# Casting the x windows on GpSimd's DMA queue and cutting the last loads and stores of a windowed matmul

**Chip and metric.** One core of a Trainium2 chip. Time is device microseconds of one execution, median of several; all runs quoted here are of the fast state (none is over 1.5% above the fastest of its kernel). The profile's span is about 1.7 us shorter than the time.

## The reference

```python
B, S, D, W = 4, 4096, 4096, 64
x: (4, 4096, 4096) fp32    w: (4096, 4096) fp32    offsets: (4,) int64, drawn at random
for b in range(B):
    o = int(offsets[b])
    results.append(x[b, o:o+W] @ w)        # 64 x 4096 by 4096 x 4096
return np.stack(results).astype(np.float32)
```

All of w (67 MB) has to be read once, and 1 MB of x per batch.

## The kernel before

The rows of two batches share the 128 partitions: `xpair[g]` holds batch 2g in partitions 0 to 63 and batch 2g+1 in 64 to 127. TensorE transposes them into fp16 `xT`. w comes as 64 tiles of 128 rows by 2048 columns, cast to fp16 by the DMA, on GpSimd's queue (67.1 MB of w read, 33.6 MB written by that queue on the page). Half of the columns is finished at a time, in eight PSUM tiles of 128x512. At most eight of GpSimd's loads are in flight, since each waits for the one eight places before (in the trace eight are issued by 6.0 us, the ninth at 6.99, when a w tile has landed).

```python
for b in range(B):                                   # x: fp32, 64 partitions each, two queues
    g, m = divmod(b, 2)
    eng = nc.sync if (b % 2 == 0) else nc.scalar
    eng.dma_start(out=xpair[g][m * WIN : (m + 1) * WIN, :],
                  in_=x[b][bass.ds(off_vals[b], WIN), :])
# ... transposes in fp32, copies PSUM -> xT (fp16) on VectorE ...
for c in range(2):
    for ki in range(n_k):                            # 32 tiles of w
        wh = wh_pool.tile([P, NH], fp16, name="wh", tag="wh")
        nc.gpsimd.dma_start(out=wh[:], in_=w[ki*KT:(ki+1)*KT, c*NH:(c+1)*NH])
        # ... 8 matmuls of 128x512 ...
    for g in range(G):
        # ... 4 copies PSUM -> stage, then two stores of 64 partitions each:
        for m in range(2):
            st_eng = nc.sync if (m == 0) else nc.scalar
            st_eng.dma_start(out=out[2*g+m][:, c*NH:(c+1)*NH],
                             in_=stage[m * WIN : (m + 1) * WIN, :])
```

Of the kernel before, what the change touches and what calls it, by code (L numbers as in the profile page):

```python
# [1 line left out]

# [5 lines left out]


@with_exitstack  # L10
def kernel(
    ctx: ExitStack,
    tc: tile.TileContext,
    x: bass.AP,
    w: bass.AP,
    offsets: bass.AP,
    out: bass.AP,
):
    nc = tc.nc
    fp32 = mybir.dt.float32  # L20
    fp16 = mybir.dt.float16

    B, S, D = x.shape
    _, N = w.shape
    WIN = out.shape[1]
    P = 128
    KT = 128
    NT = 512
    NH = N // 2
    n_k = D // KT  # L30
    n_half_sub = NH // NT
    G = B // 2

    SP = mybir.EngineType.SP
    ACT = mybir.EngineType.Activation

    const_pool = ctx.enter_context(tc.tile_pool(name="const", bufs=1))
    x_pool = ctx.enter_context(tc.tile_pool(name="xp", bufs=1))
    wh_pool = ctx.enter_context(tc.tile_pool(name="wh", bufs=18))
    st_pool = ctx.enter_context(tc.tile_pool(name="st", bufs=2))  # L40
    psum_pool = ctx.enter_context(tc.tile_pool(name="ps", bufs=1, space=bass.MemoryType.PSUM))

    identity = const_pool.tile([P, P], fp32, name="identity")
    off_t = const_pool.tile([1, B], mybir.dt.int64, name="off_t")

    xpair = [x_pool.tile([P, D], fp32, name=f"xpair{g}") for g in range(G)]
    xT = [x_pool.tile([P, D], fp16, name=f"xT{g}") for g in range(G)]

    acc = [psum_pool.tile([P, NT], fp32, name=f"acc{a}") for a in range(2 * n_half_sub)]

    nc.sync.dma_start(out=off_t[:], in_=offsets[None, :])
    make_identity(nc, identity[:])

    off_i32 = off_t.bitcast(mybir.dt.int32)
    off_vals = [
        nc.values_load(
            off_i32[0:1, 2 * b : 2 * b + 1],
            engines=[SP, ACT],
            min_val=0,
            max_val=S - WIN,  # L60
        )
        for b in range(B)
    ]

    for b in range(B):
        g, m = divmod(b, 2)
        eng = nc.sync if (b % 2 == 0) else nc.scalar
        eng.dma_start(
            out=xpair[g][m * WIN : (m + 1) * WIN, :],
            in_=x[b][bass.ds(off_vals[b], WIN), :],  # L70
        )

    for g in range(G):
        for j in range(2 * n_half_sub):
            for q in range(4):
                k = 4 * j + q
                nc.tensor.transpose(  # L77
                    out=acc[j][:, q * KT : (q + 1) * KT],
                    in_=xpair[g][:, k * KT : (k + 1) * KT],
                    identity=identity[:],  # L80
                )
            nc.vector.tensor_copy(  # L82
                out=xT[g][:, j * NT : (j + 1) * NT], in_=acc[j][:]
            )

    for c in range(2):
        for ki in range(n_k):
            wh = wh_pool.tile([P, NH], fp16, name="wh", tag="wh")
            nc.gpsimd.dma_start(  # L89
                out=wh[:],  # L90
                in_=w[ki * KT : (ki + 1) * KT, c * NH : (c + 1) * NH],
            )
            for g in range(G):
                for j in range(n_half_sub):
                    a = g * n_half_sub + j
                    nc.tensor.matmul(  # L96
                        out=acc[a][:],
                        lhsT=xT[g][:, ki * KT : (ki + 1) * KT],
                        rhs=wh[:, j * NT : (j + 1) * NT],
                        start=(ki == 0),  # L100
                        stop=(ki == n_k - 1),
                    )
        for g in range(G):
            stage = st_pool.tile([P, NH], fp32, name="stage", tag="stage")
            for j in range(n_half_sub):
                a = g * n_half_sub + j
                if c == 1 and g == 1:
                    nc.vector.tensor_copy(  # L108
                        out=stage[:, j * NT : (j + 1) * NT], in_=acc[a][:]
                    )  # L110
                else:
                    nc.scalar.copy(  # L112
                        out=stage[:, j * NT : (j + 1) * NT], in_=acc[a][:]
                    )
            for m in range(2):
                b = 2 * g + m
                st_eng = nc.sync if (m == 0) else nc.scalar
                st_eng.dma_start(
                    out=out[b][:, c * NH : (c + 1) * NH],
                    in_=stage[m * WIN : (m + 1) * WIN, :],  # L120
                )


# [1 line left out]
_INS = ['x', 'w', 'offsets']  # L125
_OUTS = [((4, 64, 4096), 'float32')]


# [23 lines left out]
```

## Time and profile before

| | before |
|---|---|
| time | 200.42 us (200.12 to 201.49) |
| first DMA traffic | 2.5 us |
| w tile 4 landed | 34.1 us |
| last w tile landed | 184.4 us |
| end of the span | 198.1 us |

"Tile 4 landed" is read from GpSimd: its load of tile 12 was held by the landing of tile 4. I use it as the mark at which x is through and w is alone. The rest of the reading stands in the prediction. One more view is wanted for later: the DMA in one-microsecond windows of the end. The columns are the stretch, its length, busy time of PE, PEld, DVE, ACT and POOL, granted clock, DMA share and GB/s.

```profile
190.00:191.00 1.00, 0.00 (x0) 0.00 (x0) 0.00 (x0) 0.00 (x0) 0.00 (x0) 0.50 0.95 229
192.00:193.00 1.00, 0.00 (x0) 0.00 (x0) 0.00 (x0) 0.00 (x0) 0.00 (x0) 0.50 0.87 246
```

Only stores move here, and the engines read nearly full (0.95 and 0.87) at 229 and 246 GB/s, little more than half of the 426 at which w is read.

### The profile page before, as it was taken

The page shows a single profiled execution, that of the slowest core. Times are in us where ns is not written, and L with a number is a line of the kernel's source. Part 1 is how long each engine was busy: PE and PEld are TensorE (multiplying, and loading weights), DVE is VectorE, ACT ScalarE, POOL GpSimd, SP SyncE. Part 2 cuts the span into 40 slices and gives each one's busy share as a digit, 9 for nine tenths or more (in the row PEclk, how much of TensorE's full clock was granted, in tenths as well). Part 3 has the DMA queues.
Part 4 walks back from the last instruction along what each step waited for, and adds up shares of the span by engine and source line. Part 5 has one row for each costly group of instructions (what it writes and reads, how often), then busy time and mean ns, then how long its engine had stood idle before and what let it go on. Part 6 is the DMA issues. An engine that isn't in the chain of part 4 may idle for free.

```text
span 198.1 us, 1402 instructions
## 1 busy us (share of the span) xinstructions
PE 131.4 (66%) x576; PEld 60.9 (31%) x576; DVE 12.9 (7%) x20; ACT 7.4 (4%) x13; POOL 34.6 (17%) x70
## 2 busy tenths in 40 slices
PE   0000949999987777777770859977777687777500
PEld 0000939444433333333320324433333233333100
DVE  0000648100000000000000000000000000000400
ACT  1100000000000000000052000000000000000400
POOL 8301002211222222221221111222222131000000
PEclk9999987999999999999998599999999999999955
DMA  4999999999999999999999999999999999999194
GB/s 69 247 257 218 239 210 213 213 214 213 213 213 215 213 213 213 214 213 213 213 215 268 352 228 214 213 214 213 213 212 214 213 214 213 214 214 203 22 235 174
DMA packets 10183, 42.02 MB, mean 212 GB/s; under 512 B 1218, under 2 KB 1218, under 8 KB 9410
## 3 DMA queue, kind: packets, MB, share of 16 engines
q0 software_dynamic: 9216, 33.56, 84.7%
q1 hardware_dynamic: 482, 4.19, 8.0%
q10 hardware_dynamic: 480, 4.19, 7.3%
q8 instruction: 4, 0.07, 0.1%
q14 instruction: 1, 0.01, 0.0%
HBM read 71.30 MB, written 4.19 MB: 381 GB/s over the span
## 4 chain that ended last, share of the span: by engine, by line
DMA 89%; POOL 2%; issue 2%; DVE 1%; PE 1%; DVEq 0%; POOLq 0%
DMA wh<-in_w_dram 89%; POOL wh L89 2%; DVE stage L108 1%; PE acc L96 1%; DVEq L147 0%; POOL identity masks.py:199 0%; POOL identity masks.py:197 0%; POOLq masks.py:199 0%; POOLq L89 0%; DVEq L108 0%; POOLq L147 0%; POOLq L136 0%
## 5 line engine op out<-in xcount | busy, mean ns | idle before, releaser
L96 PE MATMUL acc<-wh,xT 128*128 128x512 f16 x512 | 120.3, 383 | 32.0 <-DMA wh<-in_w_dram 32.0
L96 PEld LDWEIGHTS <-xT 128*128 128x128 f16 x512 | 50.2, 98 | 101.8 <-issue 47.3
L89 POOL DMA_DIRECT2D wh<-in_w_dram x64 | 34.0, 534 | 130.5 <-DMA wh<-in_w_dram 122.2
L77 PE MATMUL acc<-identity,xpair 128*128 128x128 f32 x64 | 11.2, 358 | 22.9 <-DMA xpair<-in_x_dram 22.9
L77 PEld LDWEIGHTS acc<-identity,xpair 128*128 128x128 f32 x64 | 10.8, 194 | 23.1 <-issue 23.1
L112 ACT COPY stage<-acc 128x512 f32<-128x512 f32 x12 | 6.2, 600 | 175.1 <-PE acc L96 175.0
L108 DVE COPY stage<-acc 128x512 f32<-128x512 f32 x4 | 2.5, 683 | 150.2 <-PE acc L96 150.2
L82 DVE CAST xT<-acc 128x512 f16<-128x512 f32 x16 | 10.4, 686 | 25.2 <-PE acc L77 25.1
L112 ACT ACT_TABLE_LOAD x1 | 1.3, 1283 | 4.4 <-issue 4.4
masks.py:199 POOL TENSOR_SCALAR_AFFINE_SELECT identity<-identity 128x128 f32<-128x128 f32 x1 | 0.3, 305 | 0.1
masks.py:197 POOL MEMSET identity<- 128x128 f32 x1 | 0.2, 206 | 0.3 <-POOLq L136 0.3
L136 POOL MEMSET const-float32-0.0<- 128x1 f32 x1 | 0.1, 98 | 0.3 <-issue 0.3
L136 POOL MEMSET const-bfloat16-1.0<- 128x1 bf16 x1 | 0.1, 102 | 0.0
L136 POOL MEMSET const-uint8-127<- 128x1 uint8 x1 | 0.1, 102 | 0.0
L136 POOL MEMSET const-float32-1.0<- 128x1 f32 x1 | 0.1, 98 | 0.0
## 6 DMA issues: line engine op xcount, KB each, us to landing
wh<-in_w_dram POOLq DMA_DIRECT2D x64, 512.0 KB, 19.2
xpair<-in_x_dram ACTq DMA_DIRECT2D x2, 1024.0 KB, 20.1
xpair<-in_x_dram SPq DMA_DIRECT2D x2, 1024.0 KB, 19.4
out_dram<-stage SPq DMA_DIRECT2D x4, 512.0 KB, 7.2
out_dram<-stage ACTq DMA_DIRECT2D x4, 512.0 KB, 8.6
off_t<-in_offsets_dram SPq DMA_DIRECT2D x1, 0.0 KB
```

What stands on the lines that cost most here:

```text
L77: nc.tensor.transpose(out=acc[j][:, q * KT : (q + 1) * KT], in_=xpair[g][:, k * KT : (k + 1) * KT], identity=identity[:],)
L82: nc.vector.tensor_copy(out=xT[g][:, j * NT : (j + 1) * NT], in_=acc[j][:])
L89: nc.gpsimd.dma_start(out=wh[:], in_=w[ki * KT : (ki + 1) * KT, c * NH : (c + 1) * NH],)
L96: nc.tensor.matmul(out=acc[a][:], lhsT=xT[g][:, ki * KT : (ki + 1) * KT], rhs=wh[:, j * NT : (j + 1) * NT], start=(ki == 0), stop=(ki == n ...
L108: nc.vector.tensor_copy(out=stage[:, j * NT : (j + 1) * NT], in_=acc[a][:])
L112: nc.scalar.copy(out=stage[:, j * NT : (j + 1) * NT], in_=acc[a][:])
L136: nc = _bacc.Bacc("TRN2", target_bir_lowering=False, num_devices=1)
```

## The change

It intends to shorten the two ends. At the start: two w tiles are issued first, x is cast to fp16 on its way in (it moves to GpSimd's queue, which w's casting loads use, and GpSimd then has to read the offsets, 2.8 to 5.4 us in its trace), and the transposes become fp16 matmuls against an identity. At the end: the last four row blocks of w come as 1024-column halves, so that half of the remaining columns is stored while the other half still loads. All stores become one 128-partition DMA for each pair of batches.

```diff
+    for ki in range(2):
+        pre[(0, ki)] = wh_pool.tile([P, NH], fp16, name="w2048", tag="w2048")
+        nc.gpsimd.dma_start(out=pre[(0, ki)][:], in_=w[ki*KT:(ki+1)*KT, 0:NH])
     make_identity(nc, identity[:])              # now fp16
-            engines=[SP, ACT],
+            engines=[mybir.EngineType.Pool],    # who reads the offsets
...
-        eng.dma_start(                          # x, into fp32 xpair
+        nc.gpsimd.dma_start(                    # x, into fp16 xpair
...
-                nc.tensor.transpose(out=..., in_=xpair..., identity=identity[:])
+                nc.tensor.matmul(out=..., lhsT=xpair..., rhs=identity[:], start=True, stop=True)
...
+    def store(g, c0, cw, stage):
+        eng = nc.sync if g == 0 else nc.scalar
+        eng.dma_start(out=out[2*g:2*g+2].rearrange("b r c -> (b r) c")[:, c0:c0+cw], in_=stage[:])
+    NQ = 1024
+    LAST = 4
     for c in range(2):
+        n_full = n_k if c == 0 else n_k - LAST
...
+        for h in range(NH // NQ):               # second half of the columns only
+            for ki in range(n_full, n_k):
+                wq = load(ki, NH + h * NQ, NQ)
+                # 4 matmuls
+            for g in range(G):                  # g = 0 copied by ScalarE, g = 1 by VectorE
+                # 2 copies, then store(g, NH + h * NQ, NQ, stage)
```

More of the change, by code (lines that the diff above doesn't have):

```diff
@@ L41 @@
     psum_pool = ctx.enter_context(tc.tile_pool(name="ps", bufs=1, space=bass.MemoryType.PSUM))
-    identity = const_pool.tile([P, P], fp32, name="identity")
+    identity = const_pool.tile([P, P], fp16, name="identity")
     off_t = const_pool.tile([1, B], mybir.dt.int64, name="off_t")
-    xpair = [x_pool.tile([P, D], fp32, name=f"xpair{g}") for g in range(G)]
+    xpair = [x_pool.tile([P, D], fp16, name=f"xpair{g}") for g in range(G)]
     xT = [x_pool.tile([P, D], fp16, name=f"xT{g}") for g in range(G)]
@@ L51 @@
     nc.sync.dma_start(out=off_t[:], in_=offsets[None, :])
+    pre = {}
+    for ki in range(2):
+        pre[(0, ki)] = wh_pool.tile([P, NH], fp16, name="w2048", tag="w2048")
+        nc.gpsimd.dma_start(
+            out=pre[(0, ki)][:], in_=w[ki * KT : (ki + 1) * KT, 0:NH]
+        )
     make_identity(nc, identity[:])
@@ L66 @@
         g, m = divmod(b, 2)
-        eng = nc.sync if (b % 2 == 0) else nc.scalar
-        eng.dma_start(
+        nc.gpsimd.dma_start(
             out=xpair[g][m * WIN : (m + 1) * WIN, :],
@@ L76 @@
                 k = 4 * j + q
-                nc.tensor.transpose(
+                nc.tensor.matmul(
                     out=acc[j][:, q * KT : (q + 1) * KT],
-                    in_=xpair[g][:, k * KT : (k + 1) * KT],
-                    identity=identity[:],
+                    lhsT=xpair[g][:, k * KT : (k + 1) * KT],
+                    rhs=identity[:],
+                    start=True,
+                    stop=True,
                 )
@@ L84, with load, mm @@
             )
-    for c in range(2):
-        for ki in range(n_k):
-            wh = wh_pool.tile([P, NH], fp16, name="wh", tag="wh")
-            nc.gpsimd.dma_start(
-                out=wh[:],
-                in_=w[ki * KT : (ki + 1) * KT, c * NH : (c + 1) * NH],
-            )
+    def load(ki, c0, cw):
+        t = wh_pool.tile([P, cw], fp16, name=f"w{cw}", tag=f"w{cw}")
+        nc.gpsimd.dma_start(out=t[:], in_=w[ki * KT : (ki + 1) * KT, c0 : c0 + cw])
+        return t
+    def mm(a, ki, rhs):
+        nc.tensor.matmul(
+            out=acc[a][:],
+            lhsT=xT[a // n_half_sub][:, ki * KT : (ki + 1) * KT],
+            rhs=rhs,
+            start=(ki == 0),
+            stop=(ki == n_k - 1),
+        )
@@ new lines, in store @@
+    def store(g, c0, cw, stage):
+        eng = nc.sync if g == 0 else nc.scalar
+        eng.dma_start(
+            out=out[2 * g : 2 * g + 2].rearrange("b r c -> (b r) c")[:, c0 : c0 + cw],
+            in_=stage[:],
+        )
+    NQ = 1024
+    LAST = 4
+    for c in range(2):
+        n_full = n_k if c == 0 else n_k - LAST
+        for ki in range(n_full):
+            wh = pre[(c, ki)] if (c, ki) in pre else load(ki, c * NH, NH)
+            for a in range(2 * n_half_sub):
+                j = a % n_half_sub
+                mm(a, ki, wh[:, j * NT : (j + 1) * NT])
+        if c == 0:
@@ L93 @@
             for g in range(G):
+                stage = st_pool.tile([P, NH], fp32, name="stage", tag="stage")
                 for j in range(n_half_sub):
-                    a = g * n_half_sub + j
-                    nc.tensor.matmul(
-                        out=acc[a][:],
-                        lhsT=xT[g][:, ki * KT : (ki + 1) * KT],
-                        rhs=wh[:, j * NT : (j + 1) * NT],
-                        start=(ki == 0),
-                        stop=(ki == n_k - 1),
-                    )
@@ L103 @@
-        for g in range(G):
-            stage = st_pool.tile([P, NH], fp32, name="stage", tag="stage")
-            for j in range(n_half_sub):
-                a = g * n_half_sub + j
-                if c == 1 and g == 1:
-                    nc.vector.tensor_copy(
-                        out=stage[:, j * NT : (j + 1) * NT], in_=acc[a][:]
-                    )
-                else:
-                    nc.scalar.copy(
-                        out=stage[:, j * NT : (j + 1) * NT], in_=acc[a][:]
-                    )
-            for m in range(2):
-                b = 2 * g + m
-                st_eng = nc.sync if (m == 0) else nc.scalar
-                st_eng.dma_start(
-                    out=out[b][:, c * NH : (c + 1) * NH],
-                    in_=stage[m * WIN : (m + 1) * WIN, :],
-                )
+                    nc.scalar.copy(
+                        out=stage[:, j * NT : (j + 1) * NT],
+                        in_=acc[g * n_half_sub + j][:],
+                    )
@@ new lines @@
+                store(g, 0, NH, stage)
+            continue
+        for h in range(NH // NQ):
+            js = range(h * NQ // NT, (h + 1) * NQ // NT)
+            for ki in range(n_full, n_k):
+                wq = load(ki, NH + h * NQ, NQ)
+                for g in range(G):
+                    for j in js:
+                        r = j * NT - h * NQ
+                        mm(g * n_half_sub + j, ki, wq[:, r : r + NT])
+            for g in range(G):
+                stage = st_pool.tile([P, NQ], fp32, name="stq", tag="stq", bufs=4)
+                copy = nc.scalar.copy if g == 0 else nc.vector.tensor_copy
+                for j in js:
+                    r = j * NT - h * NQ
+                    copy(out=stage[:, r : r + NT], in_=acc[g * n_half_sub + j][:])
+                store(g, NH + h * NQ, NQ, stage)
```

## The prediction

> **What bounds the kernel now.** I read the page first: engines, slices, queues, chain.
>
> ```profile
> span 198.1 us, 1402 instructions
> PE 131.4 (66%) x576; PEld 60.9 (31%) x576; DVE 12.9 (7%) x20; ACT 7.4 (4%) x13; POOL 34.6 (17%) x70
> DMA  4999999999999999999999999999999999999194
> GB/s 69 247 257 218 239 210 213 213 214 213 213 213 215 213 213 213 214 213 213 213 215 268 352 228 214 213 214 213 213 212 214 213 214 213 214 214 203 22 235 174
> DMA 89%; POOL 2%; issue 2%; DVE 1%; PE 1%; DVEq 0%; POOLq 0%
> ```
>
> The DMA row is full from the second slice to the 37th, then empty for one slice, then partly busy. The chain is 89% DMA. TensorE is busy two thirds of the time and waits for w. So the time is: start of the DMA, plus all the work queued on it until the last w tile lands, plus a tail. I priced these three.
>
> The steady price of a w tile comes from the chain in order of time. Every hop is a load issued when the load eight places earlier landed.
>
> ```profile
> 61.94 19.14 DMA wh<-in_w_dram
> 81.61 19.13 DMA wh<-in_w_dram
> 101.27 24.11 DMA wh<-in_w_dram
> 125.91 19.13 DMA wh<-in_w_dram
> ```
>
> From 61.94 to 81.61 is 19.67 us for eight tiles, 2.46 us each. A tile is 128x2048 values, 1.05 MB read as fp32 (0.52 MB written as fp16), so w is read at 426 GB/s. The hop at 101.27 holds the stores of the first half of the columns: 24.11 - 19.13 = 5.0 us for 2.1 MB, 420 GB/s. Stores that interleave with w cost about their bytes.
>
> Now the start. GpSimd's timeline: from the ninth load on, each issue marks the landing of tile 0, 1, 2 and so on.
>
> ```profile
> 1.27 0.66 POOL L89 DMA_DIRECT2D wh<-in_w_dram  x1 [0.32 <-issue]
> 6.99 0.53 POOL L89 DMA_DIRECT2D wh<-in_w_dram  x1 [0.99 <-DMA wh<-in_w_dram]
> 18.77 0.53 POOL L89 DMA_DIRECT2D wh<-in_w_dram  x1 [11.24 <-DMA wh<-in_w_dram]
> 29.45 0.53 POOL L89 DMA_DIRECT2D wh<-in_w_dram  x1 [10.15 <-DMA wh<-in_w_dram]
> 31.64 0.53 POOL L89 DMA_DIRECT2D wh<-in_w_dram  x1 [1.67 <-DMA wh<-in_w_dram]
> 34.08 0.53 POOL L89 DMA_DIRECT2D wh<-in_w_dram  x1 [1.91 <-DMA wh<-in_w_dram]
> ```
>
> Tiles 1 to 4 land between 7.0 and 34.1: 27.1 us for four tiles that should take 9.8. The other 17.3 us went to x, which shares the DMA engines. In half-microsecond windows the DMA becomes active at 2.5 us; from there to 7.0 is 4.5 us with one tile in it, so 2.0 us more (slow first moments included). The four x loads, 4.19 MB, cost 19.3 us: 217 GB/s, half the rate of w. The DMA row reads full all the while. A busy share does not show that a transfer is slow.
>
> The tail, from the timeline of the end:
>
> ```profile
> 184.45 1.89 PE L96 MATMUL acc<-wh,xT 128*128 128x512 f16 x8 [0.55 <-DMA wh<-in_w_dram]
> 184.86 2.05 ACT L112 COPY stage<-acc 128x512 f32<-128x512 f32 x4 [79.43 <-PE acc L96]
> 185.78 2.48 DVE L108 COPY stage<-acc 128x512 f32<-128x512 f32 x4 [150.18 <-PE acc L96]
> 186.94 1.82 SPq L118 DMA_DIRECT2D out_dram<-stage  x2
> 186.95 1.86 ACTq L118 DMA_DIRECT2D out_dram<-stage  x2
> ```
>
> The last tile lands at 184.4. Eight matmuls and four DVE copies reach 188.3, then 2.1 MB of stores go out alone, about 280 GB/s from 188.0 to 195.6, and the end is 198.1: 13.7 us after the last tile.
>
> [...] Each x load fills 64 partitions. [...] The trace cannot confirm a gain: interleaved half stores already cost 420 GB/s, alone 280.
> [...] Here 2.5 us lie between the last visible traffic (195.6) and the end, so I keep 2.5.
>
> **The change, part by part.**
>
> *x becomes a casting load on GpSimd's queue.* The bytes read stay 4.19 MB; those written into SBUF halve. Read side: four loads of 1.05 MB at the w price of 2.46 us are 9.8 us. [...] I take 10.7 us (estimate) against 19.3: **-8.6 us**, all of it on the path, as the DMA never idles before the last tile.
>
> *Two w tiles go first, and the offsets are read by GpSimd.* The first load is issued before the identity memset, at about 0.8 instead of 1.27: **-0.4 us**. GpSimd must then build the identity and read four offsets before it can issue x. Beside it lies the price of that on SyncE: first read at 1.9, first x issue at 4.64, so 2.7 us for four reads with checks.
>
> ```profile
> L56 SPq TENSOR_LOAD <-off_t x4: 268/272/463, 1.9 to 3.9; - x4
> ```
>
> If GpSimd reads as fast: two w issues to about 2.1, identity to about 3, reads to 5.8, first x issue there, its data 1.2 us later (as the first w: 1.27 to 2.5), at 7.0. The two w tiles, from 2.1 on with a slow first half microsecond, last 4.9 us and end at about 7.5. The hole is covered, barely. I allow **+0.8 us** for the slow start and a small hole.
>
> *fp16 transposes as plain matmuls.* TensorE's 11.2 us of them fall by several us and the first real matmul moves from 34 to about 23 us. Worth **0**: w paces the rest. TensorE needs 8 x 0.236 = 1.9 us per tile against 2.46, so it catches up in either kernel, and with 18 buffers no load waits on it in the built order before the buffers come round.
>
> *The last four rows of tiles come as half-width tiles, first half of the columns complete before the second.* Eight DMAs of half the bytes, as many descriptors each: I take **+0.2 us**. The stores of the first half, 1.05 MB, now fall largely into the last w loads and push them back by their bytes at 420 GB/s: **+2.5 us** before the last tile. After it: the third of four matmuls ends at about +0.9, two DVE copies of 0.65 reach +2.2, the store is issued there and its data flow 1.1 us later (186.94 to 188.0 before), at +3.3, ACT's own half from +2.6. 1.05 MB in all at 350 GB/s (between 280 and 420) is 3.0 us, to about +5.6, then 2.5 to the end: **+8.1**. Tail: 0.2 + 2.5 + 8.1 = 10.8 against 13.7, **-2.9 us**.
>
> *Merged stores in mid-kernel:* same bytes among w traffic already at 420 GB/s, **0**.
>
> Sum: -8.6 - 0.4 + 0.8 - 2.9 = -11.1 us. The change is thus mostly the x loads, although the diff spends most of its lines on the tail. 200.42 - 11.1 = 189.3; I say 189.2.
>
> **The rivals.**
> 1. *x stays slow.* If the 217 GB/s came [...] from how x lies in HBM, or from three queues alternating in large packets, the cast may not cure it. For it: both halves were in flight at once[...]. Against it: w is read with strides at full rate in the same stretch[...]. Cost: 19.3 again, time about 197.8, within 2%. If x shows 3.4 us a load, halfway: 192.
> 2. *A hole after the two early tiles.* GpSimd may be slower at reading offsets than SyncE, and the x issues sit behind it in one order with everything else; each us more than planned is a us lost, at most some 3: 192. For it: my plan has half a microsecond to spare.
> 3. *The tail gives nothing.* If the first half's stores just delay w and the last stores run at 280 [...], the tail is 12 to 13: 191. Conversely, if they mostly flow after the last tile while TensorE and the copies run, the 2.5 shrinks to 1: 187.5.
> 4. *TensorE becomes the bound* because PE starts with a backlog: 1.9 against 2.46 us a tile, so no.
>
> **Range and chances.** The x term carries the spread: 9.8 to about 14 us, -1 to +3. The tail adds -1.5 to +1.5, the start -0.5 to +1.5. They are independent enough that not all go one way: 186.3 to 193.3. Faster by over 2% means under 196.4, which needs rival 1 in full or several together: 0.95 for faster, 0.04 for within 2%, 0.01 for slower.
>
> **What would show each step.** In the changed profile: x landing near 10, 12, 15 and 17 us, and the first w load that waits for an x load issued soon after each (right if x takes 2.5 to 2.8 us a load, wrong at 4 or more); the DMA busy near 7 us without a gap; tile 4 landed near 26 instead of 34; w still at 2.46 us a tile; the mid hop still about 24 us; the last w tile near 179 and the end about 8 us after. The prediction is wrong if x keeps about 217 GB/s on its read side, or if a gap opens ahead of x.

## The result and the profile after

| | before | after |
|---|---|---|
| time, median | 200.32 us (15 runs) | 186.48 us (8 runs, 185.79 to 187.08) |
| ratio, 95% interval | 1 | 0.9309 (0.9287 to 0.9330) |
| tile 4 landed | 34.1 | 28.2 |
| last w tile landed | 184.4 | 178.8 |
| from there to the end | 13.7 | 6.4 |

Ratios are formed from the fast runs of the same rounds, so they are not quite the ratio of the medians. The kernel gained 13.8 us where 11.1 had been worked out: inside the range, close to its lower end. The ends gained in other shares than predicted.

The page of the changed kernel:

```profile
span 185.2 us, 1385 instructions
DMA  3999999999999999999999999999999999999975
GB/s 55 211 189 210 208 212 216 213 213 214 214 212 214 214 214 212 212 212 213 214 216 246 358 257 215 213 214 212 213 213 214 213 215 212 212 211 208 208 268 228
```

The empty slice near the end is gone. At the start, GB/s is the flat 210 of a casting load instead of 218 to 257. That is not slower: with the cast, the bytes written are counted, half of those read (33.6 MB on the page before for the 67.1 MB of w). GpSimd's timeline, where each x load's landing now releases a w load:

```profile
1.37 1.19 POOL L55 DMA_DIRECT2D w<-in_w_dram  x2 [0.80 <-POOLq L162]
13.52 0.53 POOL L96 DMA_DIRECT2D w<-in_w_dram  x1 [2.75 <-DMA xpair<-in_x_dram]
15.98 0.53 POOL L96 DMA_DIRECT2D w<-in_w_dram  x1 [1.94 <-DMA xpair<-in_x_dram]
18.41 0.53 POOL L96 DMA_DIRECT2D w<-in_w_dram  x1 [1.90 <-DMA xpair<-in_x_dram]
21.53 0.53 POOL L96 DMA_DIRECT2D w<-in_w_dram  x1 [2.60 <-DMA xpair<-in_x_dram]
28.24 0.53 POOL L96 DMA_DIRECT2D w<-in_w_dram  x1 [1.93 <-DMA w<-in_w_dram]
```

The x loads land 2.4 to 3.1 us apart, close to a w tile's 2.46. But the first lands at 13.5, not near 10, and the first w load was issued no earlier than before (1.37 against 1.27). The timeline of the end:

```profile
175.37 5.35 SPq L110 DMA_DIRECT2D out_dram<-stq  x2
...
178.88 1.02 PE L100 MATMUL acc<-w,xT 128*128 128x512 f16 x4 [0.24 <-DMA w<-in_w_dram]
...
179.72 1.29 DVE L146 COPY stq<-acc 128x512 f32<-128x512 f32 x2 [3.73 <-PE acc L100]
181.04 0.34 ACTq L110 DMA_DIRECT2D out_dram<-stq  x1
```

and the same end in windows:

```profile
176.50:177.00 0.50, 0.50 (x3) 0.19 (x2) 0.00 (x0) 0.00 (x0) 0.00 (x0) 1.00 1.06 311
177.50:178.00 0.50, 0.38 (x2) 0.19 (x2) 0.00 (x0) 0.00 (x0) 0.00 (x0) 1.00 1.00 373
180.00:180.50 0.50, 0.00 (x0) 0.00 (x0) 0.50 (x2) 0.36 (x1) 0.00 (x0) 1.00 0.14 57
182.00:183.00 1.00, 0.00 (x0) 0.00 (x0) 0.00 (x0) 0.00 (x0) 0.00 (x0) 0.99 1.01 410
```

The first half's stores are issued at 175.4 and 176.0, flow from 176.3 on (GB/s climbs over w's 210) and are nearly through by 180. The final stores move at 410 GB/s, where the kernel before had 229 and 246 in the windows shown above, 361 at most. Two things thus happened in the tail, an overlap and a faster store, and the trace alone does not share the gain out between them. Nor does it say whether x got cheaper by the cast, the queue or the order.

### The profile page after: what moved, and what is told of

It reads as the page before. It is cut to its first block, busy times and chain, and to the rows that moved or that the text cites. A ratio compares the mean times of both kernels' runs of the same rounds, so it can differ in the third digit from the quotient of the medians.

```text
span 185.2 us, 1385 instructions
## 1 busy us (share of the span) xinstructions
PE 128.4 (69%) x576; PEld 56.1 (30%) x576; DVE 12.3 (7%) x20; ACT 7.4 (4%) x13; POOL 38.8 (21%) x78
## 3 DMA queue, kind: packets, MB, share of 16 engines
HBM read 71.30 MB, written 4.19 MB: 408 GB/s over the span
## 4 chain that ended last, share of the span: by engine, by line
DMA 89%; issue 5%; POOL 1%; POOLq 1%; PE 0%; DVE 0%; DVEq 0%
DMA w<-in_w_dram 89%; POOLq L63 1%; POOL w L55 1%; PE acc L100 0%; DVE stq L146 0%; POOL xpair L74 0%; DVEq L173 0%; POOL w L96 0%; POOLq L74 0%; POOL identity masks.py:197 0%; POOLq L96 0%; POOLq masks.py:199 0%; POOLq L173 0%; POOLq L162 0%
## 5 line engine op out<-in xcount | busy, mean ns | idle before, releaser
L100 PE MATMUL acc<-w,xT 128*128 128x512 f16 x512 | 122.6, 386 | 33.6 <-DMA w<-in_w_dram 33.4
L96 POOL DMA_DIRECT2D w<-in_w_dram x66 | 34.8, 528 | 126.5 <-DMA w<-in_w_dram 113.5
L83 PE MATMUL acc<-identity,xpair 128*128 128x128 f16 x64 | 6.0, 280 | 17.9 <-DMA xpair<-in_x_dram 15.8
L146 DVE COPY stq<-acc 128x512 f32<-128x512 f32 x4 | 2.6, 686 | 151.8 <-PE acc L100 151.8
L83 PEld LDWEIGHTS <-xpair 128*128 128x128 f16 x64 | 5.6, 129 | 18.0 <-issue 18.0
L90 DVE CAST xT<-acc 128x512 f16<-128x512 f32 x16 | 9.7, 680 | 16.9 <-PE acc L83 16.9
L127 ACT COPY stage<-acc 128x512 f32<-128x512 f32 x8 | 4.0, 626 | 92.8 <-PE acc L100 92.8
L146 ACT COPY stq<-acc 128x512 f32<-128x512 f32 x4 | 2.1, 588 | 79.3 <-PE acc L100 79.3
L74 POOL DMA_DIRECT2D xpair<-in_x_dram x4 | 2.1, 518 | 3.1 <-issue 2.9
L55 POOL DMA_DIRECT2D w<-in_w_dram x2 | 1.2, 598 | 0.8 <-POOLq L162 0.8
## 6 DMA issues: line engine op xcount, KB each, us to landing
w<-in_w_dram POOLq DMA_DIRECT2D x60, 512.0 KB, 19.3
out_dram<-stage SPq DMA_DIRECT2D x1, 1024.0 KB, 11.1
```

Of the source, the lines that this page charges most:

```text
L55: nc.gpsimd.dma_start(out=pre[(0, ki)][:], in_=w[ki * KT : (ki + 1) * KT, 0:NH])
L74: nc.gpsimd.dma_start(out=xpair[g][m * WIN : (m + 1) * WIN, :], in_=x[b][bass.ds(off_vals[b], WIN), :],)
L83: nc.tensor.matmul(out=acc[j][:, q * KT : (q + 1) * KT], lhsT=xpair[g][:, k * KT : (k + 1) * KT], rhs=identity[:], start=True, stop=True,)
L90: nc.vector.tensor_copy(out=xT[g][:, j * NT : (j + 1) * NT], in_=acc[j][:])
L96: nc.gpsimd.dma_start(out=t[:], in_=w[ki * KT : (ki + 1) * KT, c0 : c0 + cw])
L100: nc.tensor.matmul(out=acc[a][:], lhsT=xT[a // n_half_sub][:, ki * KT : (ki + 1) * KT], rhs=rhs, start=(ki == 0), stop=(ki == n_k - 1),)
```

## The experiments

Eleven kernels ran, in three groups, each group on one chip with its own runs of the kernel before. All results were correct. Differences in us below are the ratio applied to the 200.3 us of before.

**1. The start alone.** The kernel before with the first three hunks of the diff; its w loop, copies and stores are as before.

```diff
-            wh = wh_pool.tile(...); nc.gpsimd.dma_start(out=wh[:], ...)
+            wh = pre[(c, ki)] if (c, ki) in pre else <the same tile and load>
```

> The start of the change (two early w tiles, x cast to fp16 on GpSimd's queue, fp16 transposes) with the tail and stores of before. My reading of the two traces: the start is worth what tile 4 gained, 34.1 to 28.2, so -5.9 us: 194.5 us, with the last 13.7 us unchanged. The recorded prediction's share for the start was -8.2 us: 192.1. Rival: the gain of the start is taken back later and only the tail counts: 199 or more.

193.14 us, ratio 0.9646 (0.9614 to 0.9678): -7.1 us. Tile 4 landed at 27.7, the last tile at 177.7 (184.4 before), and the end came 13.4 us later. So the start keeps all its gain to the end. It is worth somewhat more than I had read from one trace: there the fourth x load took 3.1 us, here all four landed 2.4 to 2.5 us apart (12.96, 15.40, 17.89, 20.32). Tile 4 shows only 6.4 of the 7.1 us, as the landings are not even. Tile 7 shows them all; its landing in the kernel before, here, and in run 4 below:

```profile
42.12 0.53 POOL L89 DMA_DIRECT2D wh<-in_w_dram  x1 [2.62 <-DMA wh<-in_w_dram]
35.04 0.53 POOL L100 DMA_DIRECT2D w<-in_w_dram  x1 [1.93 <-DMA w<-in_w_dram]
34.96 0.53 POOL L94 DMA_DIRECT2D wh<-in_w_dram  x1 [2.78 <-DMA wh<-in_w_dram]
```

**2. The end alone.** The start of before, the w loop and stores of the change.

```diff
-        wh = pre[(c, ki)] if (c, ki) in pre else load(ki, c * NH, NH)   # of the changed kernel
+        wh = load(ki, c * NH, NH)                                       # x, offsets, transposes as before
```

> The start of before, with the half-width last tiles and merged stores of the change. My reading: from the last w tile to the end 6.4 us instead of 13.7, and the last tile only 0.3 us later: -7.0 us, 193.3 us. The recorded prediction's share for the tail was -2.9: 197.4. Rival, that the two parts need each other (a smaller gain apart than together): e1 and e2 would sum to clearly less than 13.8 us.

193.28 us, ratio 0.9650 (0.9619 to 0.9681): -7.0 us. The two parts sum to -14.1, against -13.8 for the whole change: within the intervals they are independent. This run also prices the tail cleanly, as its tile 4 landed at 34.1, exactly where it did before. From its chain of waits in order of time (start, duration, what):

```profile
175.00 9.74 DMA w<-in_w_dram
184.78 0.82 PE acc L92 x3
```

The last tile landed at 184.7, 0.3 us later than in the kernel before (184.4), although 1.05 MB of stores had been issued ahead of it. From there to the end of its span, 191.5, are 6.8 us.

**3. Merged stores alone.**

```diff
-            for m in range(2):
-                st_eng.dma_start(out=out[2*g+m][:, cols], in_=stage[m*WIN:(m+1)*WIN, :])
+            st_eng = nc.sync if (g == 0) else nc.scalar
+            st_eng.dma_start(out=out[2*g:2*g+2].rearrange("b r c -> (b r) c")[:, cols], in_=stage[:])
```

> Only the stores change against before: one 128-partition store for each pair of batches in place of two 64-partition stores on two queues. Theory, that half-partition stores are slow: the final 2.1 MB go at about 400 GB/s instead of 280, 5.2 us instead of 7.5, and the span ends 1.3 us after the last traffic instead of 2.5: -2 to -3.5 us, 197 to 198.4. Rival, that [...] the tail's gain is the overlap alone: 0, 200.4. The stores in mid-kernel cost 5.0 us of w in both theories.

196.86 us, ratio 0.9831 (0.9795 to 0.9867): -3.4 us. The interval reaches across the 2% line, so the verdict on size is unclear, but it lies wholly below 1. Its DMA in windows, at the end:

```profile
189.00:190.00 1.00, 0.00 (x0) 0.00 (x0) 0.00 (x0) 0.00 (x0) 0.00 (x0) 1.00 1.09 442
190.00:191.00 1.00, 0.00 (x0) 0.00 (x0) 0.00 (x0) 0.00 (x0) 0.00 (x0) 1.00 0.99 410
191.00:192.00 1.00, 0.00 (x0) 0.00 (x0) 0.00 (x0) 0.00 (x0) 0.00 (x0) 0.86 0.93 393
```

The same 2.1 MB, the same two queues, the same moment: 390 to 440 GB/s where the kernel before had 361 at most, and run 1, with the same half-partition stores, 180 to 336 (181 to 188 us). The rows that the stores move are 8 KB in both. Taken first, the merge is half of the tail's gain; taken last, with the overlap in place, it is less (run 8). In mid-kernel, beside w, the merge gained nothing: the hop with the stores is 24.4 us, 5.3 over its 19.1 neighbours, against 5.0 before. So half-partition stores are slow alone and not beside w; no run here shows why.

**4. x over all partitions, nothing cast.** A 64 x 4096 window is contiguous, so it can be read as 128 half rows; VectorE's copies sort the halves. Queues, bytes and fp32 stay as before.

```diff
-            out=xpair[g][m * WIN : (m + 1) * WIN, :], in_=x[b][bass.ds(off_vals[b], WIN), :],
+            out=xwide[b][:],                                     # [128, 2048] fp32
+            in_=x[b][bass.ds(off_vals[b], WIN), :].rearrange("r (h c) -> (r h) c", h=2),
...
+            nc.vector.tensor_copy(out=xv[:, :, 4*t:4*t+4, m, :],
+                                  in_=acc[j].rearrange("p (q r h) -> p h q r", q=4, h=2))
```

> Before, with each fp32 x window loaded as 128 half rows over all 128 partitions instead of 64 rows over 64 (same bytes read and written, same queues, SyncE and ScalarE); VectorE sorts the halves as it copies the transposes out. [...] x costs about 10 us instead of about 17 to 19, tile 4 lands near 26 to 28 instead of 34, total 192.5 to 194.5. Rival, how x lies in HBM or three queues alternating in large packets: tile 4 stays near 34 and the total near 200. Second rival, written bytes (fp32 into SBUF beside w): also no gain here, since the written bytes are the same.

192.69 us, ratio 0.9618 (0.9588 to 0.9649): -7.7 us. GpSimd's timeline, the landings of tiles 1, 2 and 4:

```profile
12.78 0.53 POOL L94 DMA_DIRECT2D wh<-in_w_dram  x1 [5.32 <-DMA wh<-in_w_dram]
20.23 0.53 POOL L94 DMA_DIRECT2D wh<-in_w_dram  x1 [6.91 <-DMA wh<-in_w_dram]
26.76 0.53 POOL L94 DMA_DIRECT2D wh<-in_w_dram  x1 [1.93 <-DMA wh<-in_w_dram]
```

Tile 4 came at 26.8 instead of 34.1. Two rivals fall: the data lie in HBM as before, and the bytes written are the same. Three queues alternate as before too, but in smaller packets (the page counts 610 for SyncE's queue instead of 482, 64 more for each x load): what changed is the partitions of each load and with them the rows it writes, 8 KB instead of 16. This run doesn't separate the two, so the rival "large packets" is not ruled out by it.

**5. x over all partitions in the changed kernel** (the same edit, with the fp16 cast on GpSimd's queue).

```diff
-            out=xpair[g][m * WIN : (m + 1) * WIN, :],            # 64 partitions, fp16
+            out=xwide[b][:],                                     # 128 partitions, fp16
```

> The changed kernel with its x cast on GpSimd's queue, now as 128 half rows over all 128 partitions. In the trace of the changed kernel's start alone x landed every 2.4 to 2.5 us a load, already the price of a w tile of the same bytes. Theory, [...] nothing is left to gain: 186.5, within 0.5. Rival, [...] as the recorded prediction allowed (0.9 us): 185.6.

186.42 us, ratio 0.9312 (0.9293 to 0.9331), the same as the changed kernel's 0.9309. x landed at 13.00, 15.46, 17.96 and 20.39: 2.4 to 2.5 us a load, as over half of the partitions in run 1. So spreading x helps while it is written as fp32 from SyncE and ScalarE (run 4), and no longer once it is cast on GpSimd's queue. Which of the two, the cast or the queue, made the difference is not shown: no run loads x uncast over half of the partitions from GpSimd. The prediction had allowed 0.9 us over the 9.8 that four loads take at w's price, as an estimate; there was no such loss.

**6. Without the early w tiles, first attempt.**

```diff
-    for ki in range(2):
-        pre[(0, ki)] = wh_pool.tile(...); nc.gpsimd.dma_start(...)
```

> The changed kernel without the two w tiles ahead of x: GpSimd builds the identity, reads the offsets, then issues x, then all of w. Theory: the first DMA traffic comes only after the offset reads, about 5.5 to 6 us instead of 2.5, and the DMA paces everything: +3 to +3.7 us, 189.5 to 190.2. Rival, that the slow first two us of the DMA and TensorE's earlier start make up for it: within 1 us of the changed kernel, 186.5 to 187.5.

186.81 us, ratio 0.9334 (0.9310 to 0.9358), about 0.5 us over the changed kernel, though the two intervals overlap. This does not test what it was meant to. The trace shows one w load at 1.40, ahead of the offsets: the scheduler had moved it there by itself. The run prices the second early tile: a hole in the DMA between 6 and 7 us (94 GB/s instead of 213), worth half a microsecond.

**7. x truly first.** The same, with every w load held behind the last x load.

```diff
+        tc.add_manual_dep(w_inst, x_inst.name, <order only>, reason="x first")
```

> The changed kernel with all w loads held behind the four x loads (e6 had left one w tile ahead of them, hoisted by the scheduler). First x issue at about 4.6, so first traffic at about 5.8 instead of 2.5. Theory, the DMA paces everything from its first byte: about 3 us later, 189 to 190. Rival, that the slow first two us after the first issue are a ramp that any first DMA must go through and that x then has out of the way: no help, also 3 us later; that e6's small loss means early tiles hardly matter: within 1 us of the changed kernel.

189.38 us, ratio 0.9471 (0.9444 to 0.9498): 3.2 us over the changed kernel. First traffic came at 6.5 instead of 2.5 us. The early w load is needed once x sits behind the offsets on GpSimd; but the kernel before had it too, so it keeps a gain rather than making one.

**8. Half-partition stores in the changed kernel.**

```diff
-        eng.dma_start(out=out[2*g:2*g+2].rearrange(...)[:, c0:c0+cw], in_=stage[:])
+        for m in range(2):
+            eng = nc.sync if m == 0 else nc.scalar
+            eng.dma_start(out=out[2*g+m][:, c0:c0+cw], in_=stage[m*WIN:(m+1)*WIN, :])
```

> The changed kernel with each merged store put back into two 64-partition stores, one on SyncE and one on ScalarE. Theory: in the before kernel merging was worth 3.2 us for 2.1 MB of final stores; here 1.05 MB are left at the end, at about 200 to 280 GB/s instead of 400, 1.1 to 2.5 us more, plus up to 1 us at the end: +1.5 to +3, 188 to 189.5. Rival, that the overlap has made the merge needless: within 0.7, 186.5 to 187.2.

188.48 us, ratio 0.9418 (0.9389 to 0.9446): 2.2 us over the changed kernel. From the last tile to the end are 8.1 us instead of 6.4, with the final stores at 193 and 295 GB/s in their first two full microseconds. Merging still counts with the overlap in place, for the half of the bytes that is left.

**9. The start of run 4 with the end of the change.**

```diff
-    for c in range(2): ...             # run 4: w loop, copies and half stores of before
+    for c in range(2): ...             # w loop, split end and merged stores of the change
```

> The start of e4_x_all_ports (fp32 x over all partitions on SyncE and ScalarE, fp32 transposes) with the tail of the changed kernel. If start and tail add: 192.7 - 7.0 = 185.7, against 186.5 for the changed kernel; so the cast, the early tiles and the fp16 transposes would be matched by the wider x load alone. If the cast on GpSimd's queue brings something of its own: above 187.

186.29 us, ratio 0.9296 (0.9275 to 0.9317). The intervals of this and the changed kernel overlap: the same time. In this kernel x is not cast, SyncE and ScalarE issue it, so w has no offsets to wait behind on GpSimd and needs no early tiles, and the transposes are fp32. So all of the change's start is matched by one wider access pattern, and fp16 transposes add nothing that can be seen in this comparison (they were not run alone).

**10. A finer end.** Run 9 with the last 2048 columns cut into 1024, 512 and 512.

```diff
-        for h in range(NH // NQ):                       # two pieces of 1024
+        for nq in (1024, 512, 512):
```

> The best of both (e8: fp32 x over all partitions, tail of the change) with the second half of the last columns cut once more, 1024 then 512 then 512. After the last tile two matmuls and one copy each remain instead of four and two (about 0.4 + 0.65 us less) and 0.52 MB of stores instead of 1.05 (1.3 us less); eight loads in place of four cost perhaps 0.5 us more: -1 to -2 us against e8, 184.3 to 185.3. Rival, small descriptors or more DMAs in flight cost more than that: 186.5 or above.

185.98 us, ratio 0.9299 (0.9275 to 0.9323): no gain over run 9, and no loss, although the page counts 2370 packets under 2 KB where the changed kernel has 1250. The two intervals leave room for some 0.6 us either way, not for the 1 to 2 us expected. The windows suggest why:

```profile
178.00:179.00 1.00, 0.54 (x2) 0.05 (x1) 0.42 (x1) 0.59 (x1) 0.00 (x0) 1.00 1.02 410
180.00:181.00 1.00, 0.00 (x0) 0.00 (x0) 0.00 (x0) 0.00 (x0) 0.00 (x0) 1.00 1.04 395
```

The DMA is no longer idle between the last w tile and the final stores; traffic runs at 377 to 410 GB/s from 177 to 181 without a gap. That there was thus no gap left for finer pieces to close is my reading of it; it was not tested further.

**11. An earlier split.** The changed kernel with `LAST = 8`.

```diff
-    LAST = 4
+    LAST = 8
```

> The changed kernel with the last eight rows of tiles cut in two instead of the last four. The first half's stores then go out with about 10 us of w loads still queued, instead of with the last 1 us or so. Theory: stores are free at LAST = 4 because they move while the last tile's landing, matmuls and copies leave the DMA idle, so among w loads they cost their bytes, 1.05 MB at about 420 GB/s, 2.5 us: the last w tile about 2 us later and 188 to 189 in all. Rival: full-width stores do not slow w at all, because they go the other way: 186.5 to 187.

190.22 us, ratio 0.9507 (0.9479 to 0.9535): 4.0 us over the changed kernel. TensorE's timeline at the end, one row for each stretch of matmuls:

```profile
173.71 1.02 PE L100 MATMUL acc<-w,xT 128*128 128x512 f16 x4 [0.23 <-DMA w<-in_w_dram]
176.93 1.52 PE L100 MATMUL acc<-w,xT 128*128 128x512 f16 x4 [2.19 <-DMA w<-in_w_dram]
178.80 3.69 PE L100 MATMUL acc<-w,xT 128*128 128x512 f16 x12 [0.35 <-DMA w<-in_w_dram]
```

Tiles had been coming every 1.25 us; the two after 173.7 came 3.2 and 1.9 us apart, 2.6 us late in all. That is the bytes of the stores, as the theory had it, so the rival (full-width stores do not slow w) falls. It cost more than I had expected because TensorE waited, its granted clock fell to half (0.50 in the windows of 178 to 180 us), and twelve matmuls stood at the end where the changed kernel has four.

## Why the prediction was right

The time fell inside the range, near its edge, and in part by luck. The two sources of the gain (x loads that ran slower than w's, overlap at the end) held, but two sizes were off in opposite directions: the tail's error of 4.1 us alone would have led to 185.1, outside the range, and the start's error of 1.1 us the other way brought it back.

- **x, predicted -8.6: measured -7.1, too large.** The step that failed is "The four x loads, 4.19 MB, cost 19.3 us: 217 GB/s"; the 10.7 us set against it were an estimate, 9.8 at w's price and 0.9 of allowance. In run 1 tile 7 landed at 35.0. Taking off the first traffic at 2.5, eight tiles of 2.46 and four x loads at 2.45 leaves 3.1 us for the slow start and the landing (after the first traffic the DMA of the changed kernel moved 74, 66, 164, 156 and 205 GB/s in half-microsecond steps before the steady 213, although two loads were queued). I take this cost to be the same however x is loaded. The same 3.1 taken off the kernel before leaves 42.1 - 2.5 - 19.7 - 3.1 = 16.9 us for x, 248 GB/s, and off run 4 9.7 us, 431 GB/s, w's own rate (estimates; at tile 4 the same sum would give x in run 4 some 470 GB/s, faster than the 426 at which w ran steadily). The DMA view of the first 40 us of the kernel before gives the packets of the two queues that load x 44% of the engines' time, 17.6 us or 238 GB/s. I had charged the start-up to x.
- **Why x was slow, and what cured it.** Run 4 shows that the shape of the x loads was the cause, and half partitions are the likely part of it: merging the stores alone was worth 3.4 us in run 3 and undoing it cost 2.2 us in run 8, with rows of the same length. Why half partitions should be slower is not shown. A cost of writing 16 KB rows as such stays open: it fits runs 1, 4 and 5 as well, since all three write rows of 8 KB or less. That halving the written bytes is the second cure is not shown either (run 5): the queue and the order changed with the cast.
- **"w still at 2.46 us a tile": held.** Eight tiles took about 19.1 us from issue to landing in the steady stretch before and after (19.13 in both chains). What holds w at 426 GB/s is not shown here.
- **First load earlier, predicted -0.4: zero.** It was issued at 1.37 against 1.27, behind 0.6 us in which GpSimd waited for nothing shown, so taking the memset from ahead of it gained nothing. The allowance of +0.8 for a hole was not needed: the two early tiles cover the offset reads (runs 6 and 7 show what happens without).
- **fp16 transposes, predicted 0: consistent with run 9**, which is as fast with fp32 transposes. They took TensorE 6.0 us instead of 11.2; they were not tried alone.
- **Stores before the last tile, predicted +2.5, and small tiles, +0.2: measured +0.3 together** (run 2). A half-width tile is as many packets as a full one, 144: 9216 for the 64 tiles of the kernel before, 576 more in run 11 than in the changed kernel for four loads more. The step that failed is that the first half's stores "fall largely into the last w loads". They are issued after the copies (175.4 and 176.0 us) and flow from 176.3, when only about the last microsecond of w is still moving (an estimate: in the kernel before w's traffic thins out at 183.0, 1.4 us ahead of the last landing); then landing, four matmuls and two copies leave the DMA idle (a share of 0.00 from 184.5 to 188 us there), and the stores use that. The prediction's third rival had this case, 187.5 us, and I gave it too little weight. Run 11 puts the stores among w loads, and there they cost their 2.5 us.
- **After the last tile, predicted +8.1: 6.8 in run 2, 6.4 in the changed kernel.** The final stores move at 410 GB/s instead of the 350 taken, and the span ends 1.3 us after the last traffic (in run 3 about 1.9, an estimate from the DMA share of 0.32 in its last microsecond with traffic, 193 to 194 of 195.2) instead of the 2.5 taken. That 2.5 was itself too long: in windows of 0.1 us the last traffic of the kernel before is at 196.2, 1.9 us before its end, so the merge is not shown to shorten this wait. The merge was given 0 in mid-kernel, rightly, and too little here: run 3 is -3.4 us by itself.

In sum: the start gave 7.1 instead of 8.2, the tail 7.0 instead of 2.9.

## What to carry to other kernels

A full DMA row says nothing about the rate (here a share of 0.95 went with 229 GB/s in the kernel before, 1.01 with 410 in the changed one): compare GB/s with the best steady stretch of the same kernel, and look at how many partitions each slow transfer touches, and how long its rows are, before changing types or queues; here a contiguous window read as 128 half rows (-7.7 us, run 4) was worth the whole rebuilt start (-7.1, run 1). Stores near the end cost little here where they fell into the stretch in which the last loads land and are consumed (the last tile 0.3 us later in run 2) and their bytes where they fell among w loads (2.6 us in run 11), so split the last columns just late enough for that, and no finer than it takes to close the gap. When pricing a phase from landing times, take off the ramp and the landing first: here they were some 3.1 us (estimate, from run 1) that I had charged to x.
